# Value products of two attention groups split by halves of the keys into two PSUM banks

## Chip, cores and metric

The kernel runs on one core of a Trainium2 chip. The metric is the device time of one launch in microseconds (us). The engines are named as in the profile: PE is TensorE (PEld its weight loads), DVE VectorE, ACT ScalarE, POOL GpSimd, SP SyncE, which issues nearly all transfers.

## What is computed

One decoder layer over 1024 positions of width 1024, in float32: a projection, an mLSTM branch with four heads, a dilated attention branch with three groups of eight heads, gates, an output projection and a SwiGLU. The change is in the attention of the first two groups (dilation 1 and 4). For one head of one group, cut:

```python
ATTN_GROUPS = ((128, 1), (512, 4), (2048, 16))      # (window, dilation)
span = window // dilation                            # 128 steps
# queries in blocks of 128; each block sees the block before it and itself
dist = q_pos - k_pos
valid = (dist >= 0) & (dist <= span) & (key_idx >= 0)
s = einsum('brhnqd,brhnkd->brhnqk', qb, kk) * (dh ** -0.5) + bias
s = where(valid, s, -inf)
p = exp(s - max(s));  l = sum(p)
o = einsum('brhnqk,brhnkd->brhnqd', p, vv) / l       # the value products
...
wts = softmax(stack(lses))                           # the three groups are combined
y_b = sum(wts * stack(outs))
merged = g_a * (y_a @ w_proj_a) + g_b * (y_b @ w_proj_b)
```

Within a block, a query sees keys at or before it; in the block before, keys at or after its own place. So of the 128x128 block of a query block with itself, the quarter (queries 0 to 63, keys 64 to 127) is zero after the mask, and of the block before, the quarter (queries 64 to 127, keys 0 to 63).

## The kernel before

Large products (called GEMM here) run on PE as three products of split operands, `wh*mh`, `wh*ml`, `wl*mh`, so most of PE's instructions are lines 266, 267 and 268 (`run_s`). A GEMM unit (`gemm_s`) has 84 such matmuls of 512 columns. Units of queries, keys, and gates write their results to DRAM, and the attention reads them back.

The steps are listed in `ORDER`:

```python
ORDER = "m0 a00 a01 r0 m1 a10 a11 r1 m2 a20 a21 r2 c m3 g0 s0 g1 s1 g2 s2 g3 s3 g8 g9 g10 g11".split()
```

`m` is an mLSTM head (two GEMM units, a gate unit and `mlstm_core`), `a` a pair of an attention group and a half of its heads (`attn_pair`: two GEMM units, then `attn_core` twice), `r` the softmax rows, `c` the combination of the three groups (`attn_combine`), `g` a gate unit, `s` a weighted sum of the groups' outputs (`attn_sum`, lines 707 to 724: 24 products `nu = cb * nu` in line 718 and the sums in line 720). Then `merge_b` (GEMM lines 187 to 189) needs the sums of all `s`, and `merge_a` needs all heads.

This list is not the order on the engines. The framework's scheduler lays all instructions out on its own timeline, unit by unit with priorities, and fills an engine that would wait with later work that is ready. What comes out is one fixed order per engine, which the chip keeps.

`attn_core` (lines 527 to 609) goes over the eight query blocks of two heads, two blocks at a time; such a step of two blocks is called a quad here. For a quad: the scores in two PSUM banks (line 562, tag `S`), scale, bias and maximum on DVE (lines 576 to 584), the exponential on ACT (line 589), transposes on PE into a bank of tag `PT`, one for each of the two heads (line 594), their copy to SBUF on DVE (line 596), and the value products into a bank of tag `PV` (line 603). PSUM has three banks of tag `mm` for GEMMs, two `S`, two `PT` and one `PV`. The bank `PV` is shared by two quads and copied out once for both (line 608). `attn_core64` handles dilation 16 with blocks of 64; its value products (line 661) are already split over two banks, `PV` and `PT`.

`mlstm_core` takes its head in four chunks of two blocks (a = 0 to 3); each has transposes (line 880), state products (888), scores (907) and outputs (923), and after every second chunk a normalisation on DVE (lines 931 to 941) and transposes (947). It uses the same banks. Its loads and those of `attn_sum` take their SBUF buffers from one pool of six, tag `c`, in program order.

Of the kernel before, what the change touches and what calls it, by code (L numbers as in the profile page):

```python
# [13 lines left out]
AF = mybir.ActivationFunctionType  # L14
ALU = mybir.AluOpType
# [4 lines left out]
P = 128  # L20
# [20 lines left out]
def layer_kernel(ctx, tc, x, norm_mix_g, w_in, b_gate_if, conv_w, conv_b, mlstm_norm_g,  # L41
# [3 lines left out]
    ACT, DVE, POOL, PE, SP = nc.scalar, nc.vector, nc.gpsimd, nc.tensor, nc.sync  # L45
# [10 lines left out]
    def T(tag, shape, dt=F32):  # L56
        cnt[0] += 1
        return sb.tile(list(shape), dt, tag=tag, bufs=SBT[tag], name=f"{tag}{cnt[0]}")

    def PS(tag, shape=(P, 512)):  # L60
        cnt[0] += 1
        return ps.tile(list(shape), F32, tag=tag, bufs=PST[tag], name=f"p{tag}{cnt[0]}")

    def C(name, shape, dt=F32):
        return cp.tile(list(shape), dt, tag=name, name=name)
# [280 lines left out]
    def nat_view(g, tile_, half):  # L346

        d = DILS[g]
        if d == 1:
            return tile_[:, half * 512:(half + 1) * 512]  # L350
        return tile_.rearrange("p (n r) -> p r n", r=d)[:, half * d // 2:(half + 1) * d // 2, :]

    def perm_cols(g, ap512):
        d = DILS[g]
        return ap512 if d == 1 else ap512.rearrange("p (r n) -> p r n", r=d // 2)
# [12 lines left out]
    def key_blocks(g, qt):  # L368
        if g == 0:
            return [qt - 1, qt] if qt else [qt]  # L370
        if g == 1:
            return [qt - 1, qt] if qt % 2 else [qt]
        return [qt]
# [153 lines left out]
    def attn_core(Pi, g, hp, qd, kd, nm, ll):  # L527
        if g == 2:
            return attn_core64(Pi, hp, qd, kd, nm, ll)
        h0 = 4 * Pi + 2 * hp  # L530
        bt = T("bias", (P, 2, 256))
        for a in range(2):
            SP.dma_start(bt[:, a, :], bass.AP(tensor=R_d.tensor, offset=R_d.offset + (g * 8 + h0 + a) * RC * 384 + 127,
                                              ap=[[384 - 8, P // 8], [384 - 1, 8], [1, 256]]))
        nq = 2
        pv = None
        num = T("num", (P, S))
        for q0 in range(0, NT, nq):
            if q0 % 4 == 0:
                kt0 = key_blocks(g, q0)[0]  # L540
                nk = q0 + 4 - kt0
                qT, kT, vt = T("c", (P, 512)), T("c", (P, nk * P)), T("c", (P, nk, P))
                SP.dma_start(qT, qd[hp, :, q0 * P:q0 * P + 512])
                SP.dma_start(kT, kd[hp, :, kt0 * P:(kt0 + nk) * P])

                d, vd = DILS[g], va_d[Pi, g][:, hp * P:(hp + 1) * P]
                if g == 0:
                    SP.dma_start(vt, vd[kt0 * P:(kt0 + nk) * P, :].rearrange("(b p) c -> p b c", p=P))
                else:
                    for r in range(2):  # L550
                        SP.dma_start(vt[:, 2 * r:2 * r + 2, :], vd.rearrange("(b p d) c -> d p b c", d=d, p=P)[kt0 // 2 + r])

            blocks = [[(qt, b) for b in key_blocks(g, qt)] for qt in range(q0, q0 + nq)]
            width = sum(len(b) for b in blocks) * P

            sps = [PS("S") for _ in range(2)]
            o = 0
            for bl in blocks:
                qt, b0 = bl[0]
                w = len(bl) * P  # L560
                for a in range(2):
                    PE.matmul(sps[a][:, o:o + w], qT[a * 64:(a + 1) * 64, qt % 4 * P:(qt % 4 + 1) * P],
                              kT[a * 64:(a + 1) * 64, (b0 - kt0) * P:(b0 - kt0) * P + w], start=True, stop=True)
                o += w
            if q0 % 4 == 0:
                pv = PS("PV")
            pTs = []
            for a in range(2):
                c = h0 + a
                sp = sps[a]  # L570
                s = T("s", (P, 512))
                lens = [len(b) for b in blocks]
                if len(set(lens)) == 1:
                    w = lens[0] * P
                    sv = s[:, :width].rearrange("p (q w) -> p q w", w=w)
                    DVE.scalar_tensor_tensor(sv, sp[:, :width].rearrange("p (q w) -> p q w", w=w), 0.125,
                                             bt[:, a, None, 256 - w:].to_broadcast([P, nq, w]), op0=ALU.mult, op1=ALU.add)
                    DVE.tensor_reduce(nm[:, q0:q0 + nq, c:c + 1], sv, axis=AX.X, op=ALU.max, negate=True)
                else:
                    o = 0  # L580
                    for bl in blocks:
                        w = len(bl) * P
                        DVE.scalar_tensor_tensor(s[:, o:o + w], sp[:, o:o + w], 0.125, bt[:, a, 256 - w:], op0=ALU.mult, op1=ALU.add)
                        DVE.tensor_reduce(nm[:, bl[0][0], c:c + 1], s[:, o:o + w], axis=AX.X, op=ALU.max, negate=True)  # L584
                        o += w
                o = 0
                for bl in blocks:
                    qt, w = bl[0][0], len(bl) * P
                    ACT.activation(s[:, o:o + w], s[:, o:o + w], AF.Exp, bias=nm[:, qt, c:c + 1],  # L589
                                   accum_out=ll[:, qt, c:c + 1])  # L590
                    o += w
                tp = PS("PT")
                for i in range(width // P):
                    PE.transpose(tp[:, i * P:(i + 1) * P], s[:, i * P:(i + 1) * P], ident)
                pT = T("pt", (P, 512))
                DVE.tensor_copy(pT[:, :width], tp[:, :width])
                pTs.append(pT)
            i = 0
            for bl in blocks:
                o = (bl[0][0] % 4) * P  # L600
                for j, (qt, b) in enumerate(bl):
                    for a in range(2):
                        PE.matmul(pv[a * 64:(a + 1) * 64, o:o + P], vt[:, b - kt0, a * 64:(a + 1) * 64],
                                  pTs[a][:, i * P:(i + 1) * P], start=(j == 0), stop=(j == len(bl) - 1))
                    i += 1
            if (q0 + nq) % 4 == 0:
                half = (q0 + nq) // 4 - 1
                DVE.tensor_copy(nat_view(g, num, half), perm_cols(g, pv))
        SP.dma_start(nums_d[g][2 * Pi + hp], num)

    def attn_core64(Pi, hp, qd, kd, nm, ll):
# [384 lines left out]
    def attn_pair(g, Pi):  # L996
        qd = attn_unit(C_QA + g * 512 + Pi * 256, g, f"qa_d{g}{Pi}")
        kd = attn_unit(C_KA + g * 512 + Pi * 256, g, f"ka_d{g}{Pi}")
        for hp in range(2):
            attn_core(Pi, g, hp, qd, kd, nm[g], ll[g])  # L1000
# [139 lines left out]
    for half in range(2):  # L1140
# [7 lines left out]
        ssq, r = C("sqf", (P, 4, 2)), C("rmf", (P, 4))  # L1148
# [73 lines left out]
    for b, tg in ((0, "bias"), (0, "c"), (1, "u"), (1, "u")):  # L1222
        src_, i = ((w_gate, 0), (w_up, 1))[(b, "g") in fronts]
# [143 lines left out]
    for t in range(NT):  # L1367
        ssq, sd = small(2), small(1)
        for c in range(2):
            p = PS("mm")  # L1370
# [61 lines left out]
```

## Time and profile before

| what | value |
|---|---|
| time, median of three runs | 2113.3 us (2111.82 to 2117.02) |
| the profiled execution | 2115.15 us |
| its span, first to last instruction | 2113.4 us |
| PE, busy share of the span | 95% |
| DVE, ACT, POOL | 63%, 38%, 46% |
| PE products in the value products of line 603 | 216 instructions, 432 records |

A float32 matmul leaves two records on PE (two passes), a transpose or a GEMM matmul one. PE's records overlap, since the next one starts before the last one's result has left the array; the step from one start to the next is what a product costs, not its duration. A time such as 995.56 is the start, counted from the first instruction of the span.

### The profile page before, as it was taken

The page shows a single profiled execution, that of the slowest core. Times are in us where ns is not written, and L with a number is a line of the kernel's source. Part 1 is how long each engine was busy: PE and PEld are TensorE (multiplying, and loading weights), DVE is VectorE, ACT ScalarE, POOL GpSimd, SP SyncE. Part 2 cuts the span into 40 slices and gives each one's busy share as a digit, 9 for nine tenths or more (in the row PEclk, how much of TensorE's full clock was granted, in tenths as well). Part 3 has the DMA queues.
Part 4 walks back from the last instruction along what each step waited for, and adds up shares of the span by engine and source line. Part 5 has one row for each costly group of instructions (what it writes and reads, how often), then busy time and mean ns, then how long its engine had stood idle before and what let it go on. Part 6 is the DMA issues. An engine that isn't in the chain of part 4 may idle for free.

```text
span 2113.4 us, 31531 instructions
## 1 busy us (share of the span) xinstructions
PE 2013.9 (95%) x11433; PEld 1683.1 (80%) x11433; DVE 1326.1 (63%) x2337; ACT 806.6 (38%) x1726; POOL 966.4 (46%) x727
## 2 busy tenths in 40 slices
PE   6999998999999999999998899998999999999998
PEld 6999877877777677777876677896788888889996
DVE  6832348666776677667856675338655645566776
ACT  5322243343443343345433433445233233344423
POOL 3444443321432223333433756555554554568870
PEclk9999999999999999999999999999999999999999
DMA  4243344443344435655458876653333333375422
GB/s 154 83 120 111 82 135 129 132 127 126 112 131 140 139 111 140 135 184 160 128 184 272 273 230 217 239 186 103 124 96 104 110 95 98 120 247 157 146 83 80
DMA packets 264487, 303.50 MB, mean 144 GB/s; under 512 B 51353, under 2 KB 187052, under 8 KB 264332
## 3 DMA queue, kind: packets, MB, share of 16 engines
q1 hardware_dynamic: 263036, 299.26, 45.6%
q8 instruction: 90, 1.47, 0.3%
q10 hardware_dynamic: 1296, 2.23, 0.3%
q14 instruction: 65, 0.53, 0.1%
HBM read 207.35 MB, written 94.08 MB: 143 GB/s over the span
## 4 chain that ended last, share of the span: by engine, by line
PE 48%; DVE 10%; DMA 7%; issue 3%; POOL 2%; ACT 1%; SPq 1%; DVEq 0%; POOLq 0%; ACTq 0%
PE pmm L266 8%; PE pmm L267 8%; PE pmm L268 7%; PE pS L268 2%; PE pS L267 2%; PE pS L266 2%; DMA raw<-in_w_in 2%; DMA c<-num_d 1%; POOL wlo L107 1%; PE pmm L210 1%; PE pmm L209 1%; PE pmm L211 1%; PE pmm L1307 1%; PE pmm L1308 1%; PE pmm L1306 1%
## 5 line engine op out<-in xcount | busy, mean ns | idle before, releaser
L107 POOL TENSOR_TENSOR wlo<-sm,whi 128x512 fp32r<-128x512 f32 (+1 forms) x260 | 365.0, 1415 | 506.2 <-ACT whi L106 472.4
L107 POOL TENSOR_TENSOR wlo<-raw,whi 128x512 fp32r<-128x512 f32 (+3 forms) x228 | 341.3, 1510 | 388.3 <-ACT whi L106 371.5
L266 PE MATMUL pmm<-h,whi 128*128 128x512 f32 x824 | 333.7, 405 | 23.0 <-ACT u L298 14.0
L267 PE MATMUL pmm<-h,whi 128*128 128x512 f32 x824 | 330.9, 402 | 1.0 <-DVE h L231 1.0
L268 PE MATMUL pmm<-h,wlo 128*128 128x512 f32 x824 | 331.2, 402 | 0.0
L106 ACT ACTIVATE whi<-sm 128x512 fp32r<-128x512 f32 (+1 forms) x260 | 158.7, 634 | 257.8 <-PE pmm L267 125.1
L106 ACT ACTIVATE whi<-raw 128x512 fp32r<-128x512 f32 (+3 forms) x228 | 146.4, 669 | 219.6 <-issue 69.9
L266 PE MATMUL pmm<-t,whi 128*128 128x512 f32 x504 | 205.0, 407 | 11.7 <-DVE u L299 7.6
L266 PEld LDWEIGHTS pmm<-h,whi 128*128 128x128 f32 x824 | 158.5, 192 | 70.1 <-ACT u L298 17.4
L268 PE MATMUL pmm<-t,wlo 128*128 128x512 f32 x504 | 204.4, 406 | 0.0
L267 PE MATMUL pmm<-t,whi 128*128 128x512 f32 x504 | 204.1, 405 | 0.0
L267 PEld LDWEIGHTS pmm<-h,whi 128*128 128x128 f32 x824 | 157.1, 191 | 39.0 <-issue 3.6
L268 PEld LDWEIGHTS pmm<-h,wlo 128*128 128x128 f32 x824 | 156.5, 190 | 37.0 <-issue 2.5
L244 DVE TENSOR_TENSOR sm<-raw,raw 128x512 f32<-128x512 f32 x58 | 45.6, 787 | 181.9 <-DMA raw<-in_w_gate 63.1
L266 PEld LDWEIGHTS pmm<-t,whi 128*128 128x128 f32 x504 | 97.3, 193 | 37.8 <-DVE u L299 10.1
L849 DVE SCALAR_TENSOR_TENSOR c<-c,pm__329,c 128x256 f32<-128x256 f32 x192 | 110.9, 622 | 19.4 <-ACT c L847 17.3
L268 PEld LDWEIGHTS pmm<-t,wlo 128*128 128x128 f32 x504 | 96.7, 192 | 22.9 <-issue 2.2
L267 PEld LDWEIGHTS pmm<-t,whi 128*128 128x128 f32 x504 | 96.7, 192 | 22.3 <-issue 1.5
L589 ACT ACTIVATE s<-s,nm 128x256 f32<-128x256 f32 (+1 forms) x128 | 59.6, 466 | 83.7 <-DVE nm L584 52.2
L209 PE MATMUL pmm<-whi,h 128*128 128x256 f32 (+1 forms) x224 | 63.9, 292 | 6.9 <-DVE ifp L398 4.3
L211 PE MATMUL pmm<-whi,h 128*128 128x256 f32 (+1 forms) x224 | 64.2, 298 | 4.8 <-DVE h L163 3.3
L298 ACT ACTIVATE u<-pmm 128x512 f32<-128x512 f32 x54 | 31.8, 590 | 92.0 <-PE pmm L268 92.0
(541 smaller groups left out, 5081.5 us busy)
## 6 DMA issues: line engine op xcount, KB each, us to landing
raw<-in_w_in SPq DMA_DIRECT2D x74, 512.0 KB
gt_d<-e SPq DMA_DIRECT2D x48, 256.0 KB
raw<-in_w_gate SPq DMA_DIRECT2D x24, 512.0 KB
raw<-in_w_up SPq DMA_DIRECT2D x24, 512.0 KB
raw<-in_w_out SPq DMA_DIRECT2D x16, 512.0 KB
va_d<-u SPq DMA_DIRECT2D x24, 256.0 KB
s<-gt_d SPq DMA_DIRECT2D x24, 256.0 KB
qa_d<-e SPq DMA_DIRECT2D x24, 256.0 KB
```

What stands on the lines that cost most here:

```text
L106: ACT.activation(dh, src, AF.Copy)
L107: POOL.tensor_tensor(dl, src, f(dh), op=ALU.subtract)
L209: PE.matmul(p, sh, wh, start=(k == 0), stop=False)
L210: PE.matmul(p, sh, wl, start=False, stop=False)
L211: PE.matmul(p, sl, wh, start=False, stop=(k == K - 1))
L244: DVE.tensor_tensor(s1, a21, a22, op=ALU.add)
L266: PE.matmul(bank, wh[:, k, :], bh, start=start and k == 0, stop=False, skip_group_check=True)
L267: PE.matmul(bank, wh[:, k, :], bl, start=False, stop=False, skip_group_check=True)
L268: PE.matmul(bank, wl[:, k, :], bh, start=False, stop=k == 3, skip_group_check=True)
L298: ACT.activation(u2, ba, AF.Copy)
L589: ACT.activation(s[:, o:o + w], s[:, o:o + w], AF.Exp, bias=nm[:, qt, c:c + 1], accum_out=ll[:, qt, c:c + 1])
L849: DVE.scalar_tensor_tensor(y[:, m, :], xr[:, m, j:j + 256], cw[:, kt, j:j + 1], y[:, m, :], op0=ALU.mult, op1=ALU.add)
```

## The change

In `attn_core` each block's value product is cut into two by its keys: keys 0 to 63 go through partitions 0 to 63 into bank `PV`, keys 64 to 127 through partitions 64 to 127 into a bank of tag `PT`. With two heads in the two column halves, four tiles of 64x64 take part in place of two of 128x64. Where the mask leaves a quarter of zeros, the product has 64 columns in place of 128. Both banks are now filled and emptied for each quad: ACT copies the one bank to SBUF and DVE adds the other to it, in place of one DVE copy for two quads.

```diff
         nq = 2
-        pv = None
         num = T("num", (P, S))
...
-            if q0 % 4 == 0:
-                pv = PS("PV")
             pTs = []
...
-            i = 0
+            pv, i = [PS("PV"), PS("PT")], 0
             for bl in blocks:
-                o = (bl[0][0] % 4) * P
-                for j, (qt, b) in enumerate(bl):
+                o = (bl[0][0] - q0) * P
+                for (qt, b) in bl[::-1]:
+                    own, more = b == qt, len(bl) == 2
+                    ii = i + len(bl) - 1 if own else i
                     for a in range(2):
-                        PE.matmul(pv[a * 64:(a + 1) * 64, o:o + P], vt[:, b - kt0, a * 64:(a + 1) * 64],
-                                  pTs[a][:, i * P:(i + 1) * P], start=(j == 0), stop=(j == len(bl) - 1))
-                    i += 1
-            if (q0 + nq) % 4 == 0:
-                half = (q0 + nq) // 4 - 1
-                DVE.tensor_copy(nat_view(g, num, half), perm_cols(g, pv))
+                        for u in range(2):
+                            c0, c1 = (64 if own and u and more else 0), (64 if not own and not u else P)
+                            PE.matmul(pv[u][a * 64:(a + 1) * 64, o + c0:o + c1],
+                                      vt[u * 64:(u + 1) * 64, b - kt0, a * 64:(a + 1) * 64],
+                                      pTs[a][u * 64:(u + 1) * 64, ii * P + c0:ii * P + c1],
+                                      start=own, stop=not own or not more, skip_group_check=True)
+                i += len(bl)
+            dst = num[:, q0 * P:(q0 + 2) * P] if g == 0 else num.rearrange("p (n r) -> p r n", r=4)[:, q0 // 2, :]
+            ACT.activation(dst, pv[1][:, 0:2 * P], AF.Copy)
+            DVE.tensor_tensor(dst, dst, pv[0][:, 0:2 * P], op=ALU.add)
         SP.dma_start(nums_d[g][2 * Pi + hp], num)
```

All lines after this place stand 6 higher in the changed file: 266 stays, 603 becomes 607, 718 becomes 724, 735 becomes 741, 947 becomes 953; line 187 stays.

Since the scheduler lays the work out anew, the order changes on all engines from the first attention step to the gates. Three places follow.

PE, the value products of a quad of dilation 1, before (`pPV` is the bank, `pt` a head's transposed weights, `c` the values):

```order
L603 MATMUL pPV_4003<-pt_4052,c_3993 64x128 [waits DVE_49]
L594 MATMUL pPT_4100<-cs,s_4093 128x128 [waits PE_49,Activation_49]
L603 MATMUL pPV_4003<-pt_4064,c_3993 64x128 [waits DVE_49]
L603 MATMUL pPV_4003<-pt_4052,c_3993 64x128
L603 MATMUL pPV_4003<-pt_4064,c_3993 64x128
```

and now:

```order
L607 MATMUL pPV_4047<-pt_4045,c_4013 64x128 [waits DVE_49]
L607 MATMUL pPT_4048<-pt_4045,c_4013 64x64
L607 MATMUL pPV_4047<-pt_4033,c_4013 64x64
L607 MATMUL pPT_4048<-pt_4033,c_4013 64x128
L607 MATMUL pPV_4047<-pt_4045,c_4013 64x64
L607 MATMUL pPT_4048<-pt_4045,c_4013 64x128
```

Each product has become two, of 128 and of 64 columns in turn, in two banks.

PE, at the last transposes of mLSTM head 3 (`pPT<-cs,num`), the end of step m3, before:

```order
L947 MATMUL pPT_9880<-cs,num_9689 128x128
L947 MATMUL pPT_9870<-cs,num_9689 128x128 [waits DVE_49]
L947 MATMUL pPT_9880<-cs,num_9689 128x128 x2
L266 MATMUL pmm_10800<-t_813,whi_10784 128x512 [waits Activation_49]
L267 MATMUL pmm_10800<-t_814,whi_10784 128x512
L268 MATMUL pmm_10800<-t_813,wlo_10785 128x512
```

and now:

```order
L953 MATMUL pPT_10192<-cs,num_10001 128x128
L953 MATMUL pPT_10182<-cs,num_10001 128x128 [waits DVE_49]
L953 MATMUL pPT_10192<-cs,num_10001 128x128
L187 MATMUL pmm_11666<-t_11508,whi_11656 128x512 [waits Activation_49]
L188 MATMUL pmm_11666<-t_11509,whi_11656 128x512 [waits Pool_49]
L189 MATMUL pmm_11666<-t_11508,wlo_11657 128x512
```

Before, GEMM matmuls of the gates follow (223 of them up to `merge_b`); now the first matmul of `merge_b` (line 187) is the next instruction.

DVE, among the weighted sums (`c<-c,c` in line 718, now 724, is a product, in line 720, now 726, a sum), before:

```order
L720 TENSOR_TENSOR c_10238<-c_10238,c_10244 128x512 [waits DVE_49]
L735 TENSOR_TENSOR e_10857<-pmm_10844,u_10803 128x512 [waits DVE_49,PE_49]
L735 TENSOR_TENSOR e_10874<-pmm_10861,u_10816 128x512 [waits PE_49]
L718 TENSOR_TENSOR c_10251<-c_10250,c_10251 128x512 [waits DMAHW7_49,DMAHW3_49,DMAHW2_49]
L720 TENSOR_TENSOR c_10238<-c_10238,c_10251 128x512 [waits DVE_49]
L718 TENSOR_TENSOR c_10401<-c_10400,c_10401 128x512 [waits DMAHW7_49,DMAHW6_49,DMAHW5_49]
L735 TENSOR_TENSOR e_10890<-pmm_10801,u_10802 128x512 [waits DMAHW3_49,PE_49,Activation_49]
```

and now:

```order
L726 TENSOR_TENSOR c_10713<-c_10713,c_10719 128x512 [waits DVE_49]
L724 TENSOR_TENSOR c_10726<-c_10725,c_10726 128x512 [waits DMAHW5_49,DMAHW4_49,DMAHW3_49]
L726 TENSOR_TENSOR c_10713<-c_10713,c_10726 128x512 [waits DVE_49]
L724 TENSOR_TENSOR c_10734<-c_10733,c_10734 128x512 [waits DMAHW7_49,DMAHW6_49,DMAHW0_49]
L724 TENSOR_TENSOR c_10740<-c_10739,c_10740 128x512 [waits DMAHW4_49,DMAHW2_49,DMAHW1_49]
L726 TENSOR_TENSOR c_10734<-c_10734,c_10740 128x512 [waits DVE_49]
```

Before, the gates' results (line 735) stood between the sums; now no GEMM's result stands among them.

## Rows read from the trace of the kernel before

**Rows 1.** The page, part 1: engine, busy us, share of the span, instructions
```profile
PE 2013.9 (95%) x11433; PEld 1683.1 (80%) x11433; DVE 1326.1 (63%) x2337; ACT 806.6 (38%) x1726; POOL 966.4 (46%) x727
```

**Rows 2.** Busy time by stretch: start:end, length, engines, granted clock, DMA share, GB/s
```profile
425.00:800.00 375.00, 370.06 (x1981) 273.80 (x1980) 264.75 (x555) 154.98 (x429) 108.42 (x97) 1.00 0.41 126
995.60:1081.80 86.20, 85.24 (x396) 69.69 (x388) 60.79 (x126) 42.27 (x90) 35.47 (x34) 1.00 0.43 134
1081.80:1176.00 94.20, 80.35 (x318) 61.74 (x318) 60.69 (x105) 27.34 (x49) 33.34 (x24) 0.93 0.83 255
...
1750.00:1800.00 50.00, 50.00 (x217) 40.71 (x216) 28.42 (x32) 16.20 (x28) 26.33 (x19) 1.00 0.29 96
```

**Rows 3.** Timeline of PE around value products (L603): start us, us, what, records
```profile
442.19 0.43 PE L603 MATMUL pPV<-pt,c 128*64 128x128 f32 x2
442.55 0.44 PE L594 MATMUL pPT<-cs,s 128*128 128x128 f32 x2
442.92 1.09 PE L603 MATMUL pPV<-pt,c 128*64 128x128 f32 x14
443.94 0.88 PE L594 MATMUL pPT<-cs,s 128*128 128x128 f32 x6
...
756.51 0.88 PE L603 MATMUL pPV<-pt,c 128*64 128x128 f32 x12
757.31 0.88 PE L594 MATMUL pPT<-cs,s 128*128 128x128 f32 x6
```

**Rows 4.** Timeline of PE, last value products of dilation 16, four tiles of 64x64
```profile
995.10 0.27 PE L661 MATMUL pPV<-pt,c 64*64 64x64 f32 x1
...
995.12 0.27 PE L661 MATMUL pPT<-pt,c 64*64 64x64 f32 x1
...
995.56 0.22 PE L661 MATMUL pPT<-pt,c 64*64 64x64 f32 x1
995.71 0.66 PE L880 MATMUL pPT<-cs,c 128*128 128x128 f32 x4
```

**Rows 5.** Groups by line and shape on DVE and ACT, 420 to 1000: busy, mean ns
```profile
L926 ACT ACTIVATE num<-pPV 128x256 f32<-128x256 f32 x8 | 3.0, 374 | 3.5 <-PE pPV L923 3.3
...
L583 DVE SCALAR_TENSOR_TENSOR s<-pS,bias 128x256 f32<-128x256 f32 x39 | 16.1, 413 | 0.1
L608 DVE COPY num<-pPV 128x512 f32<-128x512 f32 x16 | 14.0, 877 | 10.7 <-PE pPV L603 10.7
...
L665 DVE COPY num<-pPV 128x256 f32<-128x256 f32 x8 | 4.7, 590 | 1.9 <-PE pPT L661 1.9
```

**Rows 6.** Timeline of PE, mLSTM head 3, and the steady start of `merge_b`
```profile
1027.80 1.47 PE L907 MATMUL pS<-c,c 128*128 128x256 f32 x8
...
1079.12 0.58 PE L266 MATMUL pmm<-t,whi 128*128 128x512 f32 x1
...
1193.23 0.80 PE L187 MATMUL pmm<-t,whi 128*128 128x512 f32 x1 [4.54 <-DVE s L1040]
```

**Rows 7.** Timeline of DVE: normalisation of head 3, then weighted products (L718)
```profile
1039.50 0.16 DVE L929 BATCH_NORM_AGGREGATE l_mv<-l_st 128x2 f32<-128x6 f32 x1
...
1049.78 1.38 DVE L941 TENSOR_SCALAR num<-num,l_s,l_nb 128x256 f32<-128x256 f32 x4
...
1089.68 0.69 DVE L718 TENSOR_TENSOR c<-c,c 128x512 f32<-128x512 f32 x1 [4.35 <-DMA c<-num_d]
...
1172.91 1.61 DVE L718 TENSOR_TENSOR c<-c,c 128x512 f32<-128x512 f32 x1
```

**Rows 8.** DMA issues from 1080 to 1180: count, KB each
```profile
c<-c_d SPq DMA_DIRECT2D x46, 128.0 KB
c<-num_d SPq DMA_DIRECT2D x23, 256.0 KB
gt_d<-e SPq DMA_DIRECT2D x14, 256.0 KB
...
yb_d<-c SPq DMA_DIRECT2D x8, 256.0 KB
```

## The prediction

> **What bounds the kernel now.** I read the busy shares first: PE is busy 95% of the span [rows 1]. By stretch, in the attention of the two groups that change (425 to 800) PE works 370 of 375 us and is granted the full 2.4 GHz; DVE is busy 265 us and ACT 155 [rows 2]. So there PE's own time sets the end, and every wait of the attention is filled with GEMM matmuls. The reader is to see next where that stops being so. From the last product of dilation 16 (995.56, [rows 4]) a chain runs: mLSTM head 3, then the 24 weighted products on DVE, then `merge_b`. From 1081.8 to 1176 PE idles 14 us of 94 at a mean granted 0.93 of its clock, and the DMA engines are 83% busy [rows 2]: here the chain already shows through. The GEMM units of the gates are what covers the rest of it. So two things count: PE time in the attention, and how much GEMM work is left when the chain starts.
>
> **The value products on PE.** From the starts in [rows 3], one instruction alone (2 records) takes 0.36 us to the next group's start, 12 records 0.80, 14 records 1.02. The 12 are six passes on either of two tiles, the 14 are eight on the longer one: 0.11 us a pass of 128 columns, and 0.14 to 0.16 us a group for the change to another shape. The four tiles of 64x64 in [rows 4] start within 0.02 us of one another; their last 28 records are seven on each tile, done in 0.61 us with the change of shape, so 0.06 to 0.07 a pass of 64 columns. In the new order 12 quads have a last group of 14 instructions, whose longest tile falls from 8 x 0.11 = 0.88 to 4 x (0.11 + 0.06) = 0.68, and 20 quads one of 10, from 6 x 0.11 to 0.56: together 12 x 0.2 + 20 x 0.1 = 4.4 us less. Against it, PE's order now changes between tile shapes 290 times and not 275 (counted over the whole order): 15 x 0.15 = 2.3 us more. Net 2.1 us less, between 4.4 less and 2.3 more.
>
> The upper end of that saving rests on tiles that run on while another one is still at its longer product; [rows 4], where all are of equal length, doesn't show this. The Trainium skill (TensorE: Matmul & The Clock Gate, section The mechanism) says that matmuls start and end strictly in program order; by that, a product of 64 columns next to one of 128 waits for it, the saving is nought, and the sum below is 4.4 us longer.
>
> **Emptying the banks.** Before, DVE made 16 copies of 877 ns, 14.0 us. Now ACT makes 32 copies of 256 columns at about 374 ns (12.0 us more) and DVE 32 sums between 413 and 590 ns, 13 to 19 us [rows 5]. Both engines have over 100 us free in the stretch [rows 2], so I cost this at nothing on the path as long as GEMM matmuls cover it. If the cover is gone, it is about 1 us a quad (ACT, then DVE), 32 us in all. What is queued behind: on ACT the exponentials and the GEMM evacuations, on DVE the same with the maxima.
>
> **What the order does.** This is the largest term. Each quad now holds `PV` and one of the two `PT` banks until ACT and DVE are through, so the scheduler's timeline places the quads further apart and fills with GEMM units that belong later. Counted in the two orders, up to the last product of dilation 16 PE has 3452 GEMM matmuls before and 3924 now; scores, transposes, mLSTM products are the same in number. These 472 are moved ahead, not added. A GEMM matmul costs 50/217 = 0.2304 us [rows 2], so the chain starts 108.8 us later: 995.6 + 108.8 - 2.1 = 1102.3. And of the 4032 before `merge_b` only 108 are left to cover it, in place of 580. The PE order shows the consequence: `merge_b` follows directly on head 3, and DVE's sums stand without GEMM results between them.
>
> What the chain takes then, from 995.56 to the steady start of `merge_b` at 1193.23, piece by piece [rows 4, 6, 7]:
> - To the scores of chunk 1 (1027.80): 32.2 us with 106 GEMM matmuls; now 108. Unchanged, 32.2.
> - From there to the end of chunk 2's outputs (1079.1): 51.3 us with 166 matmuls, 38.2 us; now none. Between 13.1 and 51.3. Adding what depends on each other: scores, DVE and outputs of chunk 1 some 7, the normalisation 9 (11.7 from 1039.50 to 1051.2, less the other work in it), transposes and their use 2.5, chunk 2 up to its outputs 8.5. I take 27.
> - To the second weighted product (1089.7): 10.6, a wait for a buffer and its load. Kept.
> - The other 22 steps to 1172.9: 83.2 us, 3.78 each. A step moves 512 KB, and a third of a 256 KB store: 0.61 MB, at the stretch's 255 GB/s 2.4 us; the gate stores that shared the queue [rows 8] are gone now, and the gates' weight loads with them. Between 2.4 and 3.78; load after load into six buffers stays, so I take 3.0: 66 us.
> - To `merge_b`: 20.3 (store, load, split). Kept.
>
> Sum 156 us, between 129 and 197.6. `merge_b` starts at 1102.3 + 156 = 1258.3 in place of 1193.2: 65 us later, between 38 and 107. After it the order is nearly as before, so that passes to the end. A check by PE's time: in 995.6 to 1176 it was busy 166 of 180 us [rows 2]; less 109 are 57, in 156 - 20 = 136 us, so 79 idle in place of 15. The profiled execution would go from 2115.15 to 2180, the median from 2113.3 to 2179. Products in the bare tail may run at the lower of PE's two clock levels (1.2 GHz), as the mean of 0.93 shows for the thinned stretch; a few us, within the bounds.
>
> **Rivals.**
> - *The chain doesn't shorten.* Its time is then 197.6, as if all were buffers and transfers: 2113 + 107 = 2220. For it: DVE idles for loads there, 4.35 us ahead of the step at 1089.68 [rows 7]. Against it: the queue was shared with other work.
> - *The banks bind.* PE meets an unfinished bank in each quad; with 32 us on top, 2211. Against it: 1421 GEMM matmuls now lie between the first and the last scores of the two groups, where there were 949 (counted in the orders), so each quad has more cover than before. [...]
> - *Not slower: the bare chain is short enough.* PE keeps its 2.1 us, and the chain has to fit into what was its time less the 109 us: from 91 us on downward nothing is lost, and the result is 2111. For it the middle piece must take 13 us, the waiting ahead of the sums vanish and the 22 steps take 1.15 us each, which is 530 GB/s, twice what the stretch moved. So hardly.
> - *No saving on PE* (tiles in step): 2183, inside the first range.
>
> **How the numbers follow.** The order uncovers the chain, with some shortening (2140 to 2200): 0.68; no shortening (2220): 0.14; banks bind (2211): 0.11; a stronger shortening or idle time regained, 2120 to 2140: 0.03; not slower: 0.04. The forecast is 2179. The range, to hold 8 in 10, reaches from 2142 (nearly the lowest chain) to 2218 (nearly none of it shortened). A measurement of this kernel tells some 0.3% (6 us) from no change: faster by more 0.02, within 0.02, slower 0.96.
>
> **What would show it.** Right: in the changed profile the last products of line 667 start near 1100; the weighted products (line 724) run from about 1160 to 1240, 3 us apart; PE idles some 90 us ahead of the steady `merge_b`, with DMA waits as releasers; value products take some 4 us less on PE. Wrong: if line 667 ends near 1000, the order doesn't bind as I read it; if PE shows idle time before the value products or transposes of the quads, the banks bind; if the sums come every 3.8 us again, the buffers and not the shared queue set their pace; if they come at 1.5 us, I priced the tail too high.

## Result and profile after

The changed kernel takes 2176.1 us (2173.6 to 2177.9), the kernel before 2114.3 beside it: a ratio of 1.0305, 95% interval 1.0285 to 1.0324 (the two medians alone give 1.029). Slower by 3%, 62 us. The profiled execution took 2174.7 us, its span 2172.9, so 59.5 more than the span before.

Engine totals of the changed kernel, to be read against [rows 1]:

```profile
PE 2020.2 (93%) x11865; PEld 1685.3 (78%) x11865; DVE 1326.4 (61%) x2353; ACT 823.8 (38%) x1758; POOL 962.9 (44%) x727
...
PE   6999999999999999999994299998999999999998
...
PEclk9999999999999999999997599999999999999999
```

PE worked only 6 us more than before (2013.9). Of the 59.5 us, 53 are therefore not work but idle time, and the line of 40 slices shows where: two slices at 4 and 2 tenths, with the granted clock at 7 and 5. The same in stretches (windows: from and to, length, then busy time of PE, PEld, DVE, ACT, POOL, the granted clock, the DMA share and GB/s):

```profile
425.00:1107.00 682.00, 674.93 (x4170) 516.60 (x4168) 434.31 (x895) 297.12 (x786) 226.25 (x198) 1.00 0.44 130
1107.00:1168.00 61.00, 49.23 (x223) 39.57 (x215) 43.06 (x110) 30.65 (x67) 16.20 (x21) 0.89 0.42 132
1168.00:1236.00 68.00, 6.79 (x30) 5.43 (x30) 33.88 (x76) 2.43 (x6) 0.00 (x0) 0.56 0.79 243
1236.00:1252.00 16.00, 11.95 (x35) 7.47 (x36) 3.48 (x5) 7.73 (x13) 12.35 (x10) 0.82 0.81 261
```

The attention itself runs well: PE is busy 675 of 682 us. From the last product of dilation 16 on, at 1107, PE idles 77 of 145 us. In the kernel before, the same part of the program is this window, in which PE idles 20 of 198 us:

```profile
995.60:1193.20 197.60, 177.38 (x759) 140.01 (x750) 127.67 (x236) 78.86 (x155) 84.28 (x70) 0.97 0.66 204
```

The order has 472 GEMM matmuls ahead of 1107 that used to lie behind the last product. Only 108 are left between it and `merge_b`, and the last of them starts at 1139.6.

The chain in that part, on PE's timeline (start, duration, engine, line, operation; in brackets the idle time ahead and what ended it), to be read against [rows 4, 6]:

```profile
1106.99 0.22 PE L667 MATMUL pPT<-pt,c 64*64 64x64 f32 x1
...
1139.80 1.47 PE L913 MATMUL pS<-c,c 128*128 128x256 f32 x8
...
1166.57 1.03 PE L929 MATMUL pPT<-st,s 128*128 128x257 f32 x4
...
1236.79 0.79 PE L187 MATMUL pmm<-t,whi 128*128 128x512 f32 x1 [43.55 <-ACT t L106]
...
1251.56 0.79 PE L188 MATMUL pmm<-t,whi 128*128 128x512 f32 x1 [1.71 <-POOL t L107]
```

And the weighted products on DVE, line 724 (duration least, median, most in ns, first and last start), with what its engine waited for, to be read against [rows 7]:

```profile
L724 DVE TENSOR_TENSOR c<-c,c x24: 671/692/693, 1169.5 to 1235.6; 128x512 f32<-128x512 f32 x24
its engine sat idle before it (us, times) until:
  DMA c<-num_d: 29.5, 16
```

The longest single wait of PE in the whole chain, 43.55 us, is `merge_b` waiting for a split on ACT. That split waits for its load of the sums, which is issued at 1231.7, after a wait for a product of line 724. PE's waits between 1107 and 1252 (engine, line, what ended it; us in total, times, longest):

```profile
PE pmm L187 <- ACT t L106: 44.2, 2, 43.5
PE pPT L953 <- DVE num L947: 25.2, 2, 17.0
```

The second row is head 3: the transposes of its outputs wait for the normalisation on DVE, which GEMM matmuls had covered before. Its longer wait, 17.0 us, lies beside the sums (it ends at 1191.3), which hold `merge_b` until 1236.8 in any case; only the other 8.2 us lie ahead of them.

### The profile page after: what moved, and what is told of

Same layout as the page of the kernel before. It is cut to its first block, busy times and chain, and to the rows that moved or that the text cites. A ratio compares the mean times of both kernels' runs of the same rounds, so it can differ in the third digit from the quotient of the medians.

```text
span 2172.9 us, 32369 instructions
## 1 busy us (share of the span) xinstructions
PE 2020.2 (93%) x11865; PEld 1685.3 (78%) x11865; DVE 1326.4 (61%) x2353; ACT 823.8 (38%) x1758; POOL 962.9 (44%) x727
## 5 line engine op out<-in xcount | busy, mean ns | idle before, releaser
L266 PE MATMUL pmm<-t,whi 128*128 128x512 f32 x504 | 201.8, 400 | 0.9 <-DVE u L299 0.7
L267 PE MATMUL pmm<-t,whi 128*128 128x512 f32 x504 | 201.8, 400 | 0.0
L187 PE MATMUL pmm<-t,whi 128*128 128x512 f32 x64 | 26.5, 426 | 46.1 <-ACT t L106 44.2
```

Source lines behind the costliest of these rows:

```text
L187: PE.matmul(p, wh[:, k, :], mh[:, sl], start=(k == 0), stop=False)
L266: PE.matmul(bank, wh[:, k, :], bh, start=start and k == 0, stop=False, skip_group_check=True)
L267: PE.matmul(bank, wh[:, k, :], bl, start=False, stop=False, skip_group_check=True)
```

## Experiments

**The theory:** the split is not what costs. A quad that holds a bank of tag `PT` lets the scheduler place the quads further apart; GEMM work is spent early, and the tail (head 3, sums, `merge_b`) stands bare. **Rival 1:** the split products, the join and the extra copies cost the time themselves. **Rival 2:** emptying two banks a quad holds PE up. For each kernel with another order, the number of GEMM matmuls up to the last product of dilation 16 was counted in that order and stands in its expectation; the records in the traces give the same differences. Ratios are to the kernel before, run in the same set (medians 2115.1 to 2118.3 us).

### One word in the kernel before

```diff
-                pv = PS("PV")
+                pv = PS("PT")
```

> The kernel before with one word altered: the value products of dilation 1 and 4 go to a bank of tag PT in place of PV. Products whole and paired, held for two quads and copied out once by DVE, as before: no split, no join, no extra emptying. PE's order now has 4020 GEMM matmuls up to the last product of dilation 16 (before 3452, changed 3924). Theory (a PT bank held by the quads spreads them, GEMM work is used up, the tail stands bare): the chain starts 568 x 0.2304 = 131 us later and takes 145 to 150 us in place of 197.6, so 78 to 84 us more: 2190 to 2200. Rival 1 (split and join cost the time) and rival 2 (emptying two banks a quad does): 2108 to 2120.

Measured: 2189.5 us, ratio 1.0331 (1.0315 to 1.0346), 0.5 us below the expected range. No product is split, nothing is joined, no bank is emptied more often, and the kernel loses no less than with the change. Its tail looks the same, in windows:

```profile
425.00:1135.10 710.10, 699.21 (x3834) 536.00 (x3833) 437.74 (x889) 291.04 (x768) 234.31 (x205) 1.00 0.43 128
1135.10:1186.90 51.80, 31.24 (x135) 23.72 (x127) 36.21 (x105) 23.12 (x53) 6.59 (x12) 0.80 0.39 122
1186.90:1254.10 67.20, 5.41 (x24) 4.15 (x22) 32.24 (x70) 2.10 (x4) 0.00 (x0) 0.55 0.81 237
```

and in PE's waits from 1135.1 to 1280:

```profile
PE pmm L187 <- ACT t L106: 44.2, 1, 44.2
PE pPT L947 <- DVE num L941: 28.5, 2, 17.5
```

The same two waits, 44.2 and 28.5 us where the changed kernel has 44.2 and 25.2. That speaks against rivals 1 and 2 as causes of the 60 us: the tag of a bank alone is enough to make them. It doesn't say what split and join are worth beside that.

### Two banks with whole products, and what went wrong in it

The changed kernel with whole products, a bank for each head:

```diff
             pv, i = [PS("PV"), PS("PT")], 0
...
+                        PE.matmul(pv[a][a * 64:(a + 1) * 64, o:o + P], vt[:, b - kt0, a * 64:(a + 1) * 64],
+                                  pTs[a][:, i * P:(i + 1) * P], start=(j == 0), stop=(j == len(bl) - 1))
...
-            ACT.activation(dst, pv[1][:, 0:2 * P], AF.Copy)
-            DVE.tensor_tensor(dst, dst, pv[0][:, 0:2 * P], op=ALU.add)
+            ACT.activation(dst[64:], pv[1][64:, 0:2 * P], AF.Copy)
+            DVE.tensor_copy(dst[:64], pv[0][:64, 0:2 * P])
```

> The value products of dilation 1 and 4 stay whole (128 keys, as before), but each quad takes two banks, PV and PT, one for each head, and empties both at its end: ACT the one, DVE the other. In the order PE has 3912 GEMM matmuls up to the last product of dilation 16 (before 3452, changed kernel 3924). Theory (the loss is the order, because a quad holds a PT bank): 2170 to 2182, the bare tail as in the changed kernel, the weighted products 2.6 us apart. Rival 1 (the split products and the join cost the time): 2108 to 2120, since neither is here.

Measured: 2196.1 us, ratio 1.0377 (1.0354 to 1.0400). The side is right (rival 1 is out), but it lies 14 us above the expected range. PE was busy 2039.9 us in it, 20 more than in the changed kernel. Its value products, added up from the start of each group to that of the next one, take 56.4 us in place of 37.1, which is nearly all of that; its timeline tells why:

```profile
436.55 0.49 PE L267 MATMUL pmm<-t,whi 128*128 128x512 f32 x1
436.97 0.87 PE L603 MATMUL pPT<-pt,c 128*64 128x128 f32 x6
437.77 0.66 PE L591 MATMUL pPT<-cs,s 128*128 128x128 f32 x4
```

Six records of a single head take 0.80 us to the next group's start. In the kernel before, twelve records of two heads, six on either tile, took the same 0.80. With a bank for each head the heads are placed apart in the order: all 64 groups of its value products have 6 or 8 records, of a single head, and the tile of the other head stands unused meanwhile. The experiment therefore changed two things. It was made again with the heads side by side and a bank for each of a quad's two query blocks:

```diff
+            for k, bl in enumerate(blocks):
...
+                        PE.matmul(pv[k][a * 64:(a + 1) * 64, 0:P], vt[:, b - kt0, a * 64:(a + 1) * 64],
+                                  pTs[a][:, i * P:(i + 1) * P], start=(j == 0), stop=(j == len(bl) - 1))
...
+            ACT.activation(dst[:, P:], pv[1][:, 0:P], AF.Copy)
+            DVE.tensor_copy(dst[:, :P], pv[0][:, 0:P])
```

> The first experiment again without its flaw: whole products with the two heads side by side, as before; the first query block of a quad goes to bank PV, the second to bank PT; ACT empties the one, DVE the other, each quad. 3936 GEMM matmuls up to the last product of dilation 16. Theory: as the changed kernel, 12 more GEMM matmuls (2.8 us) ahead and without the split's 2 to 4.4 us: 2176 to 2184. If the 20 us that the first experiment lay above the changed kernel were not from the heads standing apart, 2190 to 2200 again. Rival 1 (split and join): 2108 to 2120.

Measured: 2178.1 us, ratio 1.0278 (1.0263 to 1.0293), as expected. Against the changed kernel (1.0305, and 1.0274 when it was run again, below) no difference can be told: in total time the split is worth nothing that can be seen. PE was busy 2025.3 us, 5 more than in the changed kernel; its value products alone take 46.8 us, 10 more.

### One bank, emptied for each quad

The kernel before, with the bank emptied after each quad:

```diff
-            if q0 % 4 == 0:
-                pv = PS("PV")
+            pv, i = PS("PV"), 0
...
-            if (q0 + nq) % 4 == 0:
-                half = (q0 + nq) // 4 - 1
-                DVE.tensor_copy(nat_view(g, num, half), perm_cols(g, pv))
+            DVE.tensor_copy(dst, pv[:, 0:2 * P])
```

> The products of the kernel before, but the bank PV is emptied after each quad (256 columns, DVE) and not after two. 3420 GEMM matmuls up to the last product of dilation 16 (before 3452). Theory: shorter holding of PV alone moves nothing, 2108 to 2118. Rival 3 (what spreads the quads is emptying after each of them, not the PT bank): 2150 to 2180; the order already speaks against it.

Measured: 2119.1 us, ratio 1.0023 (1.0006 to 1.0039). The time is 1 us above the expected range. Emptying after each quad is not what spreads them; by the interval it costs between 1 and 8 us.

### The second bank from the GEMMs

In the changed kernel, and then with whole products a head at a time as in the first two-bank experiment:

```diff
-            pv, i = [PS("PV"), PS("PT")], 0
+            pv, i = [PS("PV"), PS("mm")], 0
```

> The changed kernel with one word altered: the second bank of a quad has tag mm in place of PT. Products split as in the changed kernel, same 32 copies on ACT and 32 sums on DVE. Up to the last product of dilation 16 PE's order has 3316 GEMM matmuls, so 716 are left as cover (before 580, changed 108). Theory: the tail is covered again, 2100 to 2116. Rival 1 (split and join cost it): 2160 to 2180. Rival 2 (emptying two banks a quad holds PE up): 2130 to 2180, with PE idle ahead of the quads' transposes or products.

> As the second kernel of this set (second bank tagged mm, same 3316 GEMM matmuls ahead), but with whole products, head by head, as in the first. The pair differs in the split and the join alone. By the sizes of the prediction the split saves PE 4.4 us of products less 2.3 us of shape changes: this kernel 2 us slower than the split one, at most 4.4, so 2102 to 2120. Rival (tiles keep in step, no saving, more shape changes): this one 2 us faster than the split one. Rival 1 (split and join cost tens of us): this one 50 to 60 us faster.

Measured: 2224.3 us (ratio 1.0512, 1.0489 to 1.0535) and 2260.6 us (1.0701, 1.0672 to 1.0730). Both expectations of the theory fell: the order was as wanted, and the time was worse than with the change. So a count of the order is not a forecast by itself. Stretches of the first of the two:

```profile
402.90:819.00 416.10, 372.25 (x2257) 275.48 (x2257) 248.69 (x535) 153.35 (x429) 87.85 (x78) 0.88 0.33 103
819.00:1068.60 249.60, 235.99 (x1480) 187.76 (x1474) 153.60 (x305) 100.91 (x280) 88.79 (x80) 0.97 0.51 140
```

From its first to its last product of dilation 1 and 4 PE idles 44 us, against 3.4 in the changed kernel (487.3 busy of 490.7), and the granted clock is 0.88 of the full one. The waits of PE there:

```profile
PE pPT L953 <- DVE num L947: 9.5, 2, 5.6
PE pS L561 <- DMA c<-ka_d: 9.0, 3, 6.8
PE pPV L607 <- DVE num L614: 6.8, 13, 0.7
```

PE waits there for the mLSTM's normalisation, for loads of the quads, and for their bank to be emptied; that the quads stand closer together in this order is the likely reason, but it wasn't tried by itself. The last product came at 1068.6, while fewer GEMM matmuls (3316) would have put it at 995.6 - 136 x 0.2304 = 964.3: 104 us late. Of these, 55 are more idle time (98 us up to there in place of 43), and 49 are PE work that takes longer. Rival 2 names a part of this only: the waits for the quads' own bank (third row) are 6.8 of the 44 us, and the time lies above the range given for it, too. The pair differs by 36 us, the way that was expected but many times the 2 to 4 us of the split; the whole products stood head by head, so it measures that flaw more than the split.

### Three banks shared by transposes and products

In the changed kernel, and then in the kernel before:

```diff
-    PST = dict(mm=3, S=2, PT=2, PV=1)
+    PST = dict(mm=3, S=2, PT=3)
...
     def PS(tag, shape=(P, 512)):
+        tag = {"PV": "PT"}.get(tag, tag)
```

> The changed kernel, split and join and all, with PT and PV made one tag of three banks. PE's order has 3727 GEMM matmuls up to the last product of dilation 16, so 305 left as cover (before 580, changed 108). Theory: the chain starts 63 us later than before and takes between 145 (changed) and 197.6 less the missing 63 us of cover, so 10 to 45 us lost: 2125 to 2160, clearly between the two kernels. Rival 1 (split and join cost the time): 2170 to 2180 unchanged. Rival 2 (waits for banks, as with the mm bank of the second experiment): above 2175, PE idle between 425 and the last product.

> The kernel before with PT and PV made one tag of three banks; nothing else. 3311 GEMM matmuls up to the last product of dilation 16, so 721 left as cover (before 580). PE idled 20 us between 995.6 and 1193.2 in the kernel before; more cover can fill at most that. Theory: 2095 to 2115, a candidate for faster than both. Rival 2 (fewer free banks make PE wait): 2120 to 2160 with PE idle ahead of the transposes.

Measured: 2164.8 us (ratio 1.0210, 1.0192 to 1.0229), between the two kernels though 5 us above the expected range, and 2101.3 us (0.9921, 0.9903 to 0.9939): **0.8% faster than the kernel before**, with no split at all. In the latter, the tail and what follows it:

```profile
948.10:1128.50 180.40, 162.86 (x705) 131.38 (x697) 130.74 (x247) 73.18 (x144) 69.21 (x58) 0.94 0.64 196
1128.50:1160.00 31.50, 30.45 (x130) 24.08 (x129) 7.95 (x13) 15.87 (x28) 18.79 (x15) 1.00 0.56 185
```

The sums end at 1128.5, 44 us earlier than before. The whole kernel gains 15 of these 44 in the profiled runs, because PE still has GEMM matmuls to do when the sums are through (busy 30 of the next 31.5 us). Up to 1128.5, though, PE idles 17.5 of 180 us, hardly less than the 20 of 198 before, so even here the tail is not fully covered. Of the 15 us, 11 are less work on PE (2003.0 from 2013.9) and 4 less idle time: the time is in the expected range, but the filling of idle time, by which the range was set, is the smaller part of the gain.

All kernels without a bank of tag `mm` in the quads, by the GEMM matmuls left at the last product of dilation 16 (times of the profiled runs, us; "sums" is the start of the last weighted product):

| kernel | left | last product | to the last of the sums | from there to the end | span |
|---|---|---|---|---|---|
| before, three shared banks | 721 | 948.1 | 180.4 | 969.9 | 2098.4 |
| one bank a quad | 612 | 990.4 | 183.2 | 941.4 | 2115.0 |
| before | 580 | 995.6 | 177.3 | 940.5 | 2113.4 |
| changed, three shared banks | 305 | 1073.3 | 156.4 | 934.9 | 2164.6 |
| heads apart in two banks | 120 | 1131.1 | 129.1 | 930.7 | 2190.9 |
| **changed** | 108 | 1107.0 | 128.6 | 937.3 | 2172.9 |
| two banks by query block | 96 | 1117.2 | 128.8 | 931.0 | 2177.0 |
| one word in before | 12 | 1135.1 | 119.0 | 930.0 | 2184.1 |

The fewer are left, the later the chain starts (but for the heads apart, whose products take longer); and what it gets shorter, at most 60 us, is less than what it starts later, up to 140.

### The price of the sums, bare and covered

Two of the three groups are left out of the weighted sums, in the changed kernel and in the one before; the changed kernel runs again beside them.

```diff
-            for g in range(3):
+            for g in range(1):
```

> The changed kernel, with two of the three groups left out of the weighted sums: 8 weighted products in place of 24, so the attention's result is that of dilation 1 alone. The order up to the last product of dilation 16 is unchanged (3924). Theory: the sums stand bare there, 2.64 us each, so 16 x 2.64 = 42 us less: 2130 to 2140. Rival 1 (split and join cost the 60 us, the tail not): 2165 to 2180.

> The kernel before with the same two groups left out of the weighted sums (8 products in place of 24). 3452 GEMM matmuls ahead, as before. Theory: there the sums are covered by GEMM work that has to run in any case; PE idled 20 us between 995.6 and 1193.2, so at most 20 us less: 2095 to 2113. Rival (the sums cost the same in both kernels, and cover means nothing): 42 us less, near 2073.

> The changed kernel itself, beside the two others: 2170 to 2180. The difference to the ninth is the price of 16 bare weighted products: 42 us by the theory, under 12 by rival 1.

Measured: 2129.6, 2101.9 and 2172.0 us (ratios 1.0079, 0.9947 and 1.0274). The same 16 weighted products cost 42.4 us in the changed kernel, and 13.2 in the one before (2115.1 in this set); by the ratios it is 41 and 11. The rows of line 724 in the changed kernel without them:

```profile
L724 DVE TENSOR_TENSOR c<-c,c x8: 676/692/693, 1168.0 to 1192.6; 128x512 f32<-128x512 f32 x8
```

They start where they did (1168.0, before it was 1169.5) and end 43 us earlier, and the whole kernel ends 42 us earlier: nothing else was waiting to take their place. In the kernel before, most of the time had GEMM work under it that has to be done in any case. Of the 57 us between the kernels in this set, 29 so lie at these 16 products. The other 28 us remain with the sums cut down. In the traces of that pair PE waits 20.0 us in the changed kernel for the normalisation of head 3, in two waits of 8.5 and 11.5, and 1.4 us in the one before. The bare head 3 is therefore the likely place of much of the 28 us; but the longer wait again lies beside the sums, and it wasn't tried by itself.

## Point by point

**The order as the largest term: right.** Last product 1102.3 predicted, 1107.0 measured; `merge_b` 1258.3 predicted, 1252 measured; median 2179 predicted, 2176 measured. The run with one word shows that the order alone is enough for the loss, and the runs with a third of the sums show that about half of it is the price of sums that lie bare.

**The start of the chain: 5 us too early, and not for the GEMM matmuls.** The step was 472 x 0.2304 less 2.1, so 106.7 us. PE's busy time up to the last product rose by 116.5 us (1069.2 from 952.7); a little less idle time (38 us up to there in place of 43) gave some of it back. Added up from the starts in the traces, the GEMM matmuls took 111.2 us more, 0.236 for each one moved; with one word changed, and whole products, 131.9 for 568, which is 0.232. Their price was nearly right. What the prediction put at nothing is the scores of the quads (line 562, now 561): the same 256 records take 60.3 us from the start of each group to that of the next one in place of 50.3, and 59.5 with one word changed. One group of each kind, first before, then in the changed kernel:

```profile
758.12 0.93 PE L562 MATMUL pS<-c,c 64*128 64x128 f32 x8
758.98 0.50 PE L266 MATMUL pmm<-h,whi 128*128 128x512 f32 x1
...
756.26 0.92 PE L561 MATMUL pS<-c,c 64*128 64x128 f32 x4
757.11 0.50 PE L268 MATMUL pmm<-t,wlo 128*128 128x512 f32 x1
```

Eight records take 0.86 us and four take 0.85 (half of them are of 256 columns in either group; the row names its first). That fits the scores of two heads side by side on the two halves of PE's rows, which the new order pulled apart; the records don't name the half. Before, 13 of 58 groups had six or eight records; in the changed kernel none of 69 has more than four, and with one word changed none of 65. The transposes of the quads (line 594, now 591) gave 2.7 us back.

**The value products: each step as sized, the net smaller, and not to be seen in the time.** The last groups, from their start to that of the transposes behind them, on PE's timeline of the changed kernel, to be read against [rows 3]:

```profile
434.79 0.32 PE L607 MATMUL pPV<-pt,c 64*64 64x128 f32 x1
...
435.49 0.66 PE L591 MATMUL pPT<-cs,s 128*128 128x128 f32 x4
...
447.03 0.32 PE L607 MATMUL pPV<-pt,c 64*64 64x128 f32 x1
...
447.84 0.55 PE L591 MATMUL pPT<-cs,s 128*128 128x128 f32 x3
```

0.70 us in place of 0.80, and 0.81 in place of 1.02: the 0.1 and 0.2 us of the prediction. All 20 groups of the one kind and all 12 of the other are within 0.01 us of these, and the 32 last groups together take 23.9 us in place of 28.3, the predicted 4.4 less. The changes of shape up to the last product, counted in the records, rose from 310 to 326, so 16 where the prediction had 15. The net can be added up too: the single products placed ahead of the last groups take 13.3 us in place of 9.8, so all value products take 37.13 us where they took 38.06. That is 0.9 us less, where the prediction had 2.1 and a range from 4.4 less to 2.3 more. Against the run with one word (39.8) it is 2.7, against the one with two banks by query block (46.8) it is 9.7; all these orders differ in more than the split, and in the total time it is not visible.

The Trainium skill (TensorE: Matmul & The Clock Gate, section The mechanism) says that matmuls start and end strictly in program order. As the prediction applied this, a product of 64 columns waits for one of 128 beside it, and the shorter group would have stayed at 0.80 us; the 0.70 speaks against that application. Whether the products end in program order can't be seen here, since the ends in the profile are modelled.

**Emptying the banks: no cost on the path, though ACT's part was sized too low.**

```profile
L613 ACT ACTIVATE num<-pPT x32: 361/499/640, 435.6 to 920.7; 128x256 f32<-128x256 f32 x32
...
L614 DVE TENSOR_TENSOR num<-num,pPV x32: 402/512/635, 436.0 to 921.3; 128x256 f32<-128x256 f32 x32
```

499 ns in place of 374 on ACT, 512 on DVE (413 to 590 predicted). PE's longest wait from 425 to 920 was 1.3 us, and it was for a GEMM's own evacuation:

```profile
PE pmm L266 <- DVE e L522: 1.3, 1, 1.3
```

So the rival "the banks bind" (2211) fell for this change. The Trainium skill (TensorEngine Tiling, section PSUM Bottleneck) says that tiling does not speed up the copy out of PSUM, which may become the bottleneck after a fourfold speed-up. Here it did not: no wait for a quad's bank is among PE's waits from 425 to 920. With the bank taken from the GEMMs, such waits showed, at 6.8 us.

**The chain, piece by piece** (us):

| piece | before | predicted | measured |
|---|---|---|---|
| last product to the scores of chunk 1 | 32.2 | 32.2 | 32.8 |
| to the end of chunk 2's outputs | 51.3 | 27 | 27.6 |
| to the second weighted product | 10.6 | 10.6 | 10.1 |
| 22 steps of the sums | 83.2 | 66 | 58.1 |
| to steady `merge_b` | 20.3 | 20.3 | 16.0 |
| sum | 197.6 | 156 | 144.6 |

The piece that was mis-sized by most is the steps: 2.64 us each, not 3.0. The estimate from bytes and the stretch's rate had given 2.4, and I had allowed for loads one after another; DVE waits 29.5 us for them in 16 waits, so this is there, but smaller. The two errors, 5 us too early a start and 11 too long a chain, have opposite signs. The mechanism is the one that was forecast; that the forecast lies only 3 us from the median is in part luck.

**The other rivals.** The chain shortened by 53 us, so 2220 is out. It didn't shrink to 91, so "not slower" is out: head 3's first piece and the 22 steps alone took 32.8 + 58.1 = 91 us.

## To carry to other kernels

A change that holds a scarce buffer longer, or one more of it, can move work that it doesn't touch: count what the order has left behind the last instruction of the changed part, and price the tail without it. The price of work in a tail is what lies bare, not what it takes: the same 16 products cost 42 us here and 13 there. A count of the order is no forecast either, though: check that the moved instructions won't wait for loads and banks in their new place (the bank taken from the GEMMs kept the cover, and lost 104 us ahead of it).

## What was not expected

- Idle time on PE cost twice. With the bank of tag `mm`, PE idled 44 of 416 us, in gaps of at most 7 us, at a mean granted clock of 0.88; PE's work then took 49 us longer up to the last product than 3316 matmuls at the price of the kernel before, and by an estimate from these rows 372 us of busy time at 0.88 in place of 1.00 account for 372 x 0.12 = 45 of them. In the bare tail the granted clock was 0.56, close to the lower of its two levels (1.2 GHz), and the first matmuls of `merge_b` still ran at a mean of 0.82 (1236 to 1252), though that stretch is short.
- What two tiles of 128x64 gain by working at once hung on their products standing side by side in the order: 12 records took 0.80 us on two tiles, and 6 records took 0.80 on one. A bank for each head was enough to pull them apart; PE was 15 us busier than with a bank for each query block (2039.9 to 2025.3), of which 10 are the value products. In the changed kernel the scores lost such a gain without an edit to them: 10 us.
- Three banks shared by transposes and products serve better than two and one kept apart: 0.8% for the kernel before. In its order the quads end 141 GEMM matmuls earlier, and PE was 11 us less busy in all (2003.0 to 2013.9). Added up from the starts, 5 of the 11 are GEMM matmuls and 4 the scores; why these became cheaper wasn't tried.
